# Two fused transformer blocks on one core: block 2's first layer norm and first feed-forward block by token tiles, the residual without GpSimd

## Chip, cores and metric

The kernel runs on 1 core of one Trainium2 chip. The metric is device time in microseconds of the whole kernel; less is better.

## What is computed

256 tokens of width 1024 go through two blocks. Block 1: RMS norm, stick-breaking attention and a short convolution, then a mixture of 32 experts. Block 2: attention (8 heads of 64) beside a gated MLP over positions, then a dense feed-forward, with a layer norm behind each of the two sums. The change touches the last lines of block 2:

```python
def swiglu_ffn(x, w_gate, w_up, w_down):
    return (jax.nn.silu(x @ w_gate) * (x @ w_up)) @ w_down
...
        mix = hybrid_mixer(x, w_in[l], attn_out_g[l], gmlp_out_g[l], gmlp_ln_g[l], gmlp_ln_b[l],
                           w_spatial[l], b_spatial[l], w_out[l])
        x = layer_norm(DEEPNORM_ALPHA * x + mix, ln1_g[l], ln1_b[l])
        ffn = swiglu_ffn(x, w_gate[l], w_up[l], w_down[l])
        x = layer_norm(DEEPNORM_ALPHA * x + ffn, ln2_g[l], ln2_b[l])
```

The feed-forward has 2816 hidden features, 22 blocks of 128.

## The kernel before

Everything is float32. A dense product is made of three: both operands are split into a rounded part and a rest (`hi_lo`, line 241: ACT copies into the rounded type, DVE subtracts), and PE adds hi*hi, hi*lo and lo*hi. The weights' halves are called `whi` and `wlo`, those of the activations `xh` and `xl`, `mh` and `ml`, `fh` and `fl`.

Weights come in tiles of one megabyte. `Feed` (line 48) lists them in the order of their use and issues the load of the next one on SP's queue as soon as a slot of the ring is free; `Split` (line 86) makes the halves a few units ahead into five buffers.

The stage of interest runs from line 1102 to the first feed-forward blocks. The 256 tokens are two tiles of 128 (`t` = 0, 1) with tokens on the partitions and the 1024 features on the free axis, in two halves of 512 (`c`). `attn_rows` (line 1105) gives the attention's part of the output projection for one tile, in units of 128 rows of the weight. `stats` (line 1121) adds it to the residual `xres` (`add_mix`), and takes mean and variance; POOL raises the variance to the power -0.5 (`rsqrt`, line 231). `normed` (line 1137) writes (x - mean) * rstd to `xn`, for tile 0 on ACT (which needs `mr`, the shifted mean, from DVE) and for tile 1 on DVE. PE transposes `xn` (`xn_t`), so that features come to the partitions, and `x3_t` applies gain and bias of the norm, which are per-partition scalars there, on ACT and DVE in turn. `hi_lo` then splits each chunk of 128 features over all 256 tokens, and `dense_feat` (line 258) multiplies it into the gate and the up block of the first 128 hidden features (`zg`, `zu`), chunk after chunk. `warm` (line 211) issues products that nothing reads.

The feed-forward needs the normed x once more as its own residual, by tokens. So POOL loads the four vectors of the two norms, spread over all partitions, with its own DMA queue (line 1191) and computes gain and bias on `xn` again into `xres` (lines 1193 and 1194):

```python
        for n, o in bc.items():
            nc.gpsimd.dma_start(out=o, in_=a[n].partition_broadcast(P))
        for t in range(NT):
            nc.gpsimd.tensor_tensor(out=xres[:, t, :], in0=xn[:, t, :], in1=bc["ln1_g"], op=ALU.mult)
            nc.gpsimd.tensor_tensor(out=xres[:, t, :], in0=xres[:, t, :], in1=bc["ln1_b"], op=ALU.add)
```

From there `hidden(f)` (line 1210) makes one block of 128 hidden features, gate and up, 24 products of 256 columns each, and `rows_proj` the down projection of two such blocks (`fdn`). At the end `last_rows`, `stats` and two passes on DVE give the second norm, tile by tile.

Inside `tc.manual_schedule` the engines named there keep the order of the source; what stands outside is placed by the scheduler, which may put an instruction ahead of ones written earlier.

Of the kernel before, what the change touches and what calls it, by code (L numbers as in the profile page):

```python
# [36 lines left out]
WARM3 = (6, 6)  # L37
# [10 lines left out]
class Feed:  # L48
    """Weight tiles of one megabyte each, loaded in the order of their use into the free slots."""
# [36 lines left out]
class Split:  # L86
    """Halves of weight tiles as hi + lo, made ahead of their use."""
# [28 lines left out]
def fused_blocks(ctx: ExitStack, tc: tile.TileContext, a, out):  # L116
# [28 lines left out]
    def in_halves(src):  # L145
        return [(slice(h * 1024, (h + 1) * 1024), src[:, h * 1024:(h + 1) * 1024]) for h in range(2)]

# [22 lines left out]
    for i in (2, 3, 0, 1):  # L170
        tiles(units_b, "wo2", [a["w_out_2"][i]])
    for i in range(12):
        if i < 11:
            tiles(units_b, "fgu", [a["w_ffn"][2 * i], a["w_ffn"][2 * i + 1]])
        if i:
            tiles(units_b, "fdn", [a["w_fdn"][i - 1]])

# [99 lines left out]
    def rows_proj(W, name, acc, xh, xl, k0, first, last, then={}):  # L277
        """acc[t][c] += x[:, two chunks from k0] @ w, w with 1024 columns."""
# [57 lines left out]
    def x_rstd(t):  # L336
        """1 / rms of a token tile of x, half of it on each engine."""
# [136 lines left out]
    def feat_pair(name, z):  # L474
        """z[128, 2, 256]: two blocks of 128 features of one projection."""
# [66 lines left out]
    with tc.manual_schedule(engines={mybir.EngineType.PE}):  # L542
# [31 lines left out]
        def x1_t(t, b):  # L574
            """Half b of x1 of token tile t as [d, tok]."""
# [28 lines left out]
    # what routing keeps per token goes where the router's weights were  # L604
# [62 lines left out]
    def first_max(vals, eq, nm):  # L667
        """One-hot of the first maximum along the last axis, into eq, and the maximum."""
# [13 lines left out]
    # the two best experts of each group, and the best group  # L682
# [33 lines left out]
    def gather(pg):  # L716
        """The tokens of a group of experts as [d, slots], normalised; some chunks of d at a time."""
# [16 lines left out]
    def scatter(g, pg):  # L734
        """[slots, tok]: the weight with which a slot's output goes to its token."""
# [13 lines left out]
    # the weights: softmax over the two experts, times the group's share  # L749
# [95 lines left out]
    # experts with more tokens than slots: the tokens beyond them, on all of the expert's weights  # L845
# [61 lines left out]
    def x2_tok(t, c):  # L907
        """ALPHA * x2 of token tile t, back as [tok, d]."""
# [80 lines left out]
    def soft_a(hp):  # L989
        """Scores with the mask, and their maxima."""  # L990
# [67 lines left out]
    def then(*steps):  # L1058
        """What follows a unit of weights: steps[i] after unit i."""
        return {i: (lambda fs=fs: [f(*a) for f, *a in fs]) for i, fs in enumerate(steps)}  # L1060
# [53 lines left out]
    # residual, layer norm  # L1114
# [3 lines left out]
    bc = {n: fp.tile([P, D], F32, name=n) for n in ("ln1_g", "ln1_b", "ln2_g", "ln2_b")}  # L1118
# [18 lines left out]
    def normed(t):  # L1137
        for c in range(2):
            cols = slice(c * 512, (c + 1) * 512)
            if t:  # L1140
                ts(xn[:, t, cols], xres[:, t, cols], *ln[t], op0=ALU.subtract, op1=ALU.mult)
            else:
                act(xn[:, t, cols], xres[:, t, cols], AF.Identity, scale=ln[t][1], bias=shift[t])

    with tc.manual_schedule(engines=in_order):
        zvs = [bank_c().rearrange("p (k s) -> p k s", k=2) for _ in range(4)]

        def xn_t(t, kc):
            tr(zvs[kc % 4][:, kc // 4, t * P:(t + 1) * P], xn[:, t, kc * P:(kc + 1) * P], ident)

        for c in range(2):
            attn_rows(0, (3,), (c,))
            stats(0, c, add_mix)
        attn_rows(1, (0, 1), (0, 1))
        W.ahead(W.n_got + 2)
        shift = {0: small(fp, 1, "mr")}
        stt(out=shift[0], in0=ln[0][0], scalar=-1.0, in1=ln[0][1], op0=ALU.mult, op1=ALU.mult)
        normed(0)
        for c in range(2):
            attn_rows(1, (2, 3), (c,))  # L1160
            stats(1, c, add_mix)
        warm(bank, WARM3[0], ident)
        for kc in range(KD):
            xn_t(0, kc)
        normed(1)
        warm(bank, WARM3[1], ident)
        x3 = {}

        def x3_t(kc):
            if kc >= KD:  # L1170
                return
            zv = zvs[kc % 4][:, kc // 4, :]
            x3[kc] = fp.tile([P, S], F32, tag="x3", name="x3", bufs=4)
            if kc % 2:
                act(x3[kc], zv, AF.Identity, scale=V("ln1_g", kc), bias=V("ln1_b", kc))
            else:
                ts(x3[kc], zv, V("ln1_g", kc), V("ln1_b", kc), op0=ALU.mult, op1=ALU.add)

        gate, up = W.get("fgu", 3), W.get("fgu", 4)
        zg, zu = bank()[:, 0:S], bank()[:, 0:S]  # L1180
        for kc in range(KD):
            xn_t(1, kc)
            if kc < 2:
                x3_t(kc)
        for kc in range(KD):
            hi_lo(xh[:, kc, :], xl[:, kc, :], x3[kc])
            x3_t(kc + 2)
            dense_feat(*gate, KD, xh, xl, zg, [kc])
            dense_feat(*up, KD, xh, xl, zu, [kc])
        for n, o in bc.items():  # L1190
            nc.gpsimd.dma_start(out=o, in_=a[n].partition_broadcast(P))
        for t in range(NT):
            nc.gpsimd.tensor_tensor(out=xres[:, t, :], in0=xn[:, t, :], in1=bc["ln1_g"], op=ALU.mult)
            nc.gpsimd.tensor_tensor(out=xres[:, t, :], in0=xres[:, t, :], in1=bc["ln1_b"], op=ALU.add)
        W.ahead(W.n_got + W.n)

# [20 lines left out]
    for i in range(12):  # L1217
        if i < 11:
# [4 lines left out]
            hidden(2 * i + 1)  # L1223
        if 0 < i < 10:
# [6 lines left out]
    # the last two pairs of chunks together, so that one half of the tokens is done early  # L1231
# [6 lines left out]

    for t in range(NT):
# [8 lines left out]
        mu, r = ln[t]  # L1248
        stt(out=xn[:, t, :], in0=xres[:, t, :], scalar=mu, in1=bc["ln2_g"], op0=ALU.subtract, op1=ALU.mult)
        for cols in (slice(0, 512), slice(512, 768), slice(768, D))[:2 + t]:  # L1250
            if not t:
                cols = slice(cols.start, cols.start + 512)
            o = xn[:, t, cols]
            stt(out=o, in0=o, scalar=r, in1=bc["ln2_b"][:, cols], op0=ALU.mult, op1=ALU.add)
# [8 lines left out]
def layout(i):  # L1263
    import numpy as np

    def chunks(w, n):
        """(K, F) -> (F/n, 128, K/128, n): column blocks, rows by partition."""
# [71 lines left out]
```

## Time and profile before

| | |
|---|---|
| runs | 716.70, 719.25, 719.62 us |
| median | 719.25 us |
| profiled execution | span 717.7 us (the page lists no other time for it) |
| PE busy | 665.7 us, 93% of the span |
| DVE busy | 343.9 us, 48% |
| ACT busy | 267.5 us, 37% |
| POOL busy | 58.1 us, 8% |
| mean granted clock of PE | 0.974 |

The share of an engine is a mean over stages with different limits, so what a stage waits for is read in that stage. A profile's timeline gives the start and the length of each instruction, in brackets the idle time of its engine before it and what ended that; a granted clock of 1.00 is 2.4 GHz on PE, 0.50 is 1.2 GHz. Ends of products on PE are modelled, so the distance of two starts tells more than the length of one.

### The profile page before, as it was taken

What the parts mean: (1) busy time and instruction counts of PE and PEld (TensorE: products, weight loads), DVE (VectorE), ACT (ScalarE), POOL (GpSimd) and SP (SyncE); (2) the same over time, 40 slices, a digit from 0 to 9 for tenths busy, and PEclk for the clock granted to TensorE, in tenths of its full rate; (3) what the DMA queues carried; (4) which work ended last, traced back from release to release, by engine and by line L of the source; (5) the groups of instructions that cost most, each with busy time, mean ns of one, the idle gap of its engine ahead of it and who ended that gap; (6) DMA issues with size and microseconds to landing.
All of it is one profiled execution on the core that took longest, in us unless ns stands there. A gap on an engine that the chain in (4) does not pass through costs nothing. (4 is left out here: it accounts for less than half of the span.)

```text
span 717.7 us, 11083 instructions
## 1 busy us (share of the span) xinstructions
PE 665.7 (93%) x4593; PEld 537.0 (75%) x4593; DVE 343.9 (48%) x532; ACT 267.5 (37%) x409; POOL 58.1 (8%) x68
## 2 busy tenths in 40 slices
PE   7999999999999889897799399999889999999995
PEld 6888999999964444442355288877789999999994
DVE  6657555555521220211000568676885555555556
ACT  6567554444310000000001564485554444444440
POOL 2321100000000000000000015101520000000001
PEclk9999999999999999999899799999979999999998
DMA  9983479639889999999999874632445555550001
GB/s 344 403 334 126 149 305 344 242 118 370 334 341 397 421 419 419 420 419 418 419 419 415 358 283 141 224 126 110 176 174 179 177 186 196 199 183 1 1 1 58
DMA packets 27560, 185.66 MB, mean 259 GB/s; under 512 B 3312, under 2 KB 3824, under 8 KB 5872
## 3 DMA queue, kind: packets, MB, share of 16 engines
q1 hardware_dynamic: 26928, 182.79, 65.7%
q0 software_dynamic: 576, 2.10, 0.8%
q8 instruction: 38, 0.62, 0.4%
q14 instruction: 18, 0.15, 0.1%
HBM read 183.83 MB, written 1.05 MB: 258 GB/s over the span
## 5 line engine op out<-in xcount | busy, mean ns | idle before, releaser
L243 DVE TENSOR_TENSOR wlo<-w,whi 128x1024 fp32r<-128x1024 f32 (+1 forms) x151 | 184.3, 1225 | 128.0 <-ACT whi L242 127.5
L242 ACT ACTIVATE whi<-w 128x1024 fp32r<-128x1024 f32 (+1 forms) x151 | 158.6, 1055 | 199.4 <-PE pa_t L255 75.0
L263 PE MATMUL pc_t<-xl,whi 128*128 128x256 f32 x464 | 132.2, 285 | 0.0
L262 PE MATMUL pc_t<-xh,whi 128*128 128x256 f32 x464 | 132.2, 285 | 0.0
L264 PE MATMUL pc_t<-xh,wlo 128*128 128x256 f32 x464 | 131.9, 285 | 0.0
L262 PEld LDWEIGHTS pc_t<-xh,whi 128*128 128x128 f32 x464 | 90.1, 194 | 0.4
L263 PEld LDWEIGHTS pc_t<-xl,whi 128*128 128x128 f32 x464 | 90.0, 194 | 0.4
L264 PEld LDWEIGHTS pc_t<-xh,wlo 128*128 128x128 f32 x464 | 89.8, 194 | 0.0
L780 PE MATMUL pc_t<-w,xg 128*32 128x512 f32 x512 | 62.0, 616 | 5.5 <-DMA w<-in_w_gu_dram 5.4
L810 ACT ACTIVATE h<-pc_t 128x256 f32<-128x256 f32 x8 | 3.1, 383 | 136.7 <-PE pc_t L729 112.0
L730 DVE TENSOR_TENSOR xg<-pc_t,vec 128x512 f32<-128x512 f32 (+2 forms) x18 | 11.4, 632 | 81.7 <-PE pc_t L729 81.7
L255 PE MATMUL pa_t<-whi,xh 128*128 128x512 f32 x112 | 44.8, 400 | 1.3 <-ACT xh L246 1.3
L780 PEld LDWEIGHTS pc_t<-w,xg 128*32 128x32 f32 x512 | 14.3, 111 | 40.8 <-issue 24.7
L255 PE MATMUL pa_t<-whi,xl 128*128 128x512 f32 x112 | 44.0, 392 | 0.0
L255 PE MATMUL pa_t<-wlo,xh 128*128 128x512 f32 x112 | 43.8, 391 | 0.0
L821 PEld LDWEIGHTS pa_t<-st,y 128*128 128x128 f32 x128 | 23.0, 189 | 21.9 <-DVE y L837 12.5
L821 PE MATMUL pa_t<-st,y 128*128 128x256 f32 x128 | 31.9, 392 | 6.3 <-DVE y L837 6.2
L263 PE MATMUL pa_t<-xl,whi 128*128 128x256 f32 x112 | 33.1, 295 | 5.0 <-DVE xl L243 4.9
L729 PEld LDWEIGHTS pc_t<-pr,xres 128*128 128x128 f32 x256 | 29.3, 192 | 8.4 <-PE pc_t L780 4.2
L780 PE MATMUL pc_t<-w,hT 128*32 128x512 f32 (+1 forms) x272 | 31.2, 574 | 4.1 <-ACT hT L816 4.1
L262 PE MATMUL pa_t<-xh,whi 128*128 128x256 f32 x112 | 32.8, 293 | 0.0
L264 PE MATMUL pa_t<-xh,wlo 128*128 128x256 f32 x112 | 32.4, 290 | 0.0
(296 smaller groups left out, 1042.0 us busy)
## 6 DMA issues: line engine op xcount, KB each, us to landing
w<-in_w_gu_dram SPq DMA_DIRECT2D x64, 1024.0 KB, 19.8
w<-in_w_dn_dram SPq DMA_DIRECT2D x32, 1024.0 KB, 19.9
w<-in_w_in_dram SPq DMA_DIRECT2D x28, 1024.0 KB, 14.5
w<-in_w_ffn_dram SPq DMA_DIRECT2D x22, 1024.0 KB, 5.0
w<-in_w_fdn_dram SPq DMA_DIRECT2D x11, 1024.0 KB, 5.0
w<-in_w_out_dram SPq DMA_DIRECT2D x8, 1024.0 KB, 6.1
w<-in_w_in_dram SPq DMA_DIRECT2D x4, 512.0 KB, 12.2
w<-in_w_cv_dram SPq DMA_DIRECT2D x2, 1024.0 KB, 9.6
```

What stands on the lines that cost most here:

```text
L242: act(hi, src, AF.Copy)
L243: tt(out=lo, in0=src, in1=hi.bitcast(F32), op=ALU.subtract)
L255: mm(acc[c], x_[:, kc, tok], w_[:, o + c * 512:o + (c + 1) * 512], start=first and i == 0 and n == 0, stop=last and i == len(ks) - 1 and n ...
L262: mm(acc, hi[:, f], xh[:, kc, :], start=kc == 0, stop=False)
L263: mm(acc, hi[:, f], xl[:, kc, :], start=False, stop=False)
L264: mm(acc, lo[:, f], xh[:, kc, :], start=False, stop=kc == nk - 1)
L729: mm(zv[:, k, :], xres[:, t, kc * P:(kc + 1) * P], pr[:, t, :], start=t == 0, stop=t == 1)
L730: tt(out=xg[:, ks, :], in0=zv, in1=V("ffn_g")[:, ks].unsqueeze(2).to_broadcast([P, n, P]), op=ALU.mult)
L780: mm(out[sl, 0:n], x[:, sl], w[:, e * 512 + i * n:e * 512 + (i + 1) * n], start=start, stop=stop, skip_group_check=True)
L810: act(h, gu[:, 0:256], AF.Silu)
L821: mm(acc[2 * c + k // 2][:, k % 2, :], ys[c][:, k * P:(k + 1) * P], st, start=False, stop=False, skip_group_check=True)
```

## The change

- The vectors of the norms come on SP's queue: two tiles of one megabyte, `ln1` (gain and bias) ahead of the first `fgu` tile and `ln2` behind the last `fdn` tile. `ln1` keeps its slot of the ring until its last use.
- POOL's four residual operations go. For tile 0, DVE does them (`xn` times gain, plus bias) in the loop of the feed-forward, written behind the second pass of that loop's `hidden` calls. For tile 1, DVE normalises by tokens: `centred` gives (x - mean) * gain into `xn`, `scaled` that times rstd plus bias, in quarters of 256 features, straight into `xres`; PE transposes `xres`, and no gain or bias is left to apply.
- Tile 0 is normalised on ACT as before and transposed between the two halves of tile 1's projection; gain and bias of its chunks are applied on ACT alone (`part0`).
- The first gate/up block is done for one token tile after the other (`first_hidden`, 128 columns a product): four pairs of chunks for tile 0, then four for tile 1.
- The products that nothing reads at this place (`WARM3`) go.
- The second norm's passes use the new helpers.

```diff
-WARM3 = (6, 6)
...
+    def on_all(g, b):
+        return [(slice(i * D, (i + 1) * D), a[n].partition_broadcast(P)) for i, n in enumerate((g, b))]
...
+    tiles(None, "ln1", [on_all("ln1_g", "ln1_b")])
     for i in range(12):
...
+    tiles(None, "ln2", [on_all("ln2_g", "ln2_b")])
...
+    def centred(t, cols, gain):
+        stt(out=xn[:, t, cols], in0=xres[:, t, cols], scalar=ln[t][0], in1=gain[:, cols],
+            op0=ALU.subtract, op1=ALU.mult)
+
+    def scaled(o, t, cols, bias):
+        stt(out=o, in0=xn[:, t, cols], scalar=ln[t][1], in1=bias[:, cols], op0=ALU.mult, op1=ALU.add)
...
+        W.ahead(W.n_got + 1)
         for c in range(2):
             attn_rows(0, (3,), (c,))
             stats(0, c, add_mix)
+        shift = small(fp, 1, "mr")
+        stt(out=shift, in0=ln[0][0], scalar=-1.0, in1=ln[0][1], op0=ALU.mult, op1=ALU.mult)
         attn_rows(1, (0, 1), (0, 1))
         W.ahead(W.n_got + 2)
-        shift = {0: small(fp, 1, "mr")}
-        stt(out=shift[0], in0=ln[0][0], scalar=-1.0, in1=ln[0][1], op0=ALU.mult, op1=ALU.mult)
-        normed(0)
-        for c in range(2):
-            attn_rows(1, (2, 3), (c,))
-            stats(1, c, add_mix)
-        warm(bank, WARM3[0], ident)
-        for kc in range(KD):
-            xn_t(0, kc)
-        normed(1)
-        warm(bank, WARM3[1], ident)
...
+        for cols in half:
+            act(xn[:, 0, cols], xres[:, 0, cols], AF.Identity, scale=ln[0][1], bias=shift)
+        attn_rows(1, (2, 3), (0,))
+        stats(1, 0, add_mix)
...
+        z0 = [turned(0, xn, k, 4) for k in (0, 4)]
+        attn_rows(1, (2, 3), (1,))
...
+        def part0(j):
+            x3 = fp.tile([P, 2, P], F32, tag="x3", name="x3", bufs=2)
+            for i in range(2):
+                kc = 2 * j + i
+                act(x3[:, i, :], z0[kc // 4][:, kc % 4, :], AF.Identity, scale=V("ln1_g", kc), bias=V("ln1_b", kc))
+            ks = slice(2 * j, 2 * j + 2)
+            hi_lo(xh[:, ks, tok[0]], xl[:, ks, tok[0]], x3)
+
+        def first_hidden(t, j):
+            for (hi, lo), z in ((gate, zg), (up, zu)):
+                for kc in (2 * j, 2 * j + 1):
+                    f = slice(kc * P, (kc + 1) * P)
+                    for n, (w_, x_) in enumerate(((hi, xh), (hi, xl), (lo, xh))):
+                        mm(z[:, tok[t]], w_[:, f], x_[:, kc, tok[t]], start=t == 0 and kc == 0 and n == 0,
+                           stop=kc == KD - 1 and n == 2, skip_group_check=True)
...
+        part0(0)
+        stats(1, 1, add_mix)
+        part0(1)
+        centred(1, half[0], g1)
+        part0(2)
+        centred(1, half[1], g1)
+        part0(3)
+        for j in range(4):
+            first_hidden(0, j)
+        z1 = []
+        for j in range(4):
+            scaled(xres[:, 1, quarter[j]], 1, quarter[j], b1)
+            z1.append(turned(1, xres, 2 * j, 2))
+            ks = slice(2 * j, 2 * j + 2)
+            hi_lo(xh[:, ks, tok[1]], xl[:, ks, tok[1]], z1[j])
+            if j:
+                first_hidden(1, j - 1)
+        first_hidden(1, 3)
         W.ahead(W.n_got + W.n)
...
             hidden(2 * i + 1)
+        if i == 1:
+            tt(out=xres[:, 0, :], in0=xn[:, 0, :], in1=g1, op=ALU.mult)
+            tt(out=xres[:, 0, :], in0=xres[:, 0, :], in1=b1, op=ALU.add)
+            feed.done(ln1)
```

`turned(t, src, k, n)` transposes n chunks of 128 features of a tile into one bank. The new lines shift the numbers: `add_mix` is L1139 in the changed kernel, the statistics L1130 to L1135, `hi_lo`'s subtraction L248, `first_hidden`'s products L1191, `centred` and `scaled` L1142 and L1146, tile 0's residual on DVE L1244 and L1245.

DVE in the changed kernel, from the first sum of token tile 1 to its `centred` (`w` is the tile with gain and bias, `x` a pair of chunks of tile 0):

```order
L1139 SCALAR_TENSOR_TENSOR xres<-pa_t,rs_34_5772,xres 128x512
L1244 TENSOR_TENSOR xres<-xn_5778,w 128x1024
L1130 BN_STATS bst<-xres 128x6
L248 TENSOR_TENSOR xl_4917<-x_5847,xh_4916 128x2x128
L1139 SCALAR_TENSOR_TENSOR xres<-pa_t,rs_34_5772,xres 128x512
L1245 TENSOR_TENSOR xres<-xres,w 128x1024
L1130 BN_STATS bst<-xres 128x6
L1133 BN_AGGR mv_5854<-bst 128x2
L1135 TENSOR_SCALAR ve_5856<-mv_5854 128x1
L248 TENSOR_TENSOR xl_4917<-x_5860,xh_4916 128x2x128
L1142 SCALAR_TENSOR_TENSOR xn_5778<-xres,mv_5854,w 128x512
```

The two residual operations of tile 0, written behind the second pass of the feed-forward loop, stand in the statistics of tile 1. In the kernel before, DVE has the same place without them:

```order
L1135 SCALAR_TENSOR_TENSOR xres<-pa_t,rs_34_5771,xres 128x512
L1126 BN_STATS bst<-xres 128x6
L1135 SCALAR_TENSOR_TENSOR xres<-pa_t,rs_34_5771,xres 128x512
L1126 BN_STATS bst<-xres 128x6
L1129 BN_AGGR mv_5844<-bst 128x2
L1131 TENSOR_SCALAR ve_5846<-mv_5844 128x1
L1141 TENSOR_SCALAR xn_5777<-xres,mv_5844,rs_41_5848 128x512 x2
L1177 TENSOR_SCALAR x_5877<-pc_t,vec 128x256
```

So two passes over 128x1024 moved in, and the first split of tile 0 (L248) moved ahead of tile 1's second sum.

PE in the kernel before, from the end of the projection to the first products of the gate block:

```order
L255 MATMUL pa_t<-whi,ml_4919 128x512
L215 MATMUL pa_t<-ident 128x128 x6
L1149 MATMUL pc_t<-ident,xn_5777 128x128 x8
L215 MATMUL pa_t<-ident 128x128 x6
L1149 MATMUL pc_t<-ident,xn_5777 128x128 x8
L262 MATMUL pa_t<-xh_4916,whi 128x256
```

and in the changed kernel, from tile 0's transposes on:

```order
L1169 MATMUL pc_t<-ident,xn_5778 128x128 x8
L260 MATMUL pa_t<-whi,mh_4918 128x512
L260 MATMUL pa_t<-wlo,mh_4918 128x512
L260 MATMUL pa_t<-whi,ml_4919 128x512
L260 MATMUL pa_t<-whi,mh_4918 128x512
L260 MATMUL pa_t<-wlo,mh_4918 128x512
L260 MATMUL pa_t<-whi,ml_4919 128x512
L1191 MATMUL pa_t<-xh_4916,whi 128x128
```

The transposes of tile 0 moved ahead of the last six products of the projection, the products that nothing reads are gone, and the gate block begins with tile 0 alone, at 128 columns.

## Rows read from the trace of the kernel before

**Rows 1.** span line; waits from 507 to 527: total us, times, longest

```profile
core 0 of [0], span 717.7 us
...
PE pa_t L263 <- DVE xl L243: 4.9, 4, 1.5
```

**Rows 2.** stretches: us, busy (count) of PE, PEld, DVE, ACT, POOL; PEclk, DMA, GB/s

```profile
516.70:520.17 3.47, 1.18 (x7) 0.98 (x8) 3.47 (x4) 2.27 (x4) 3.39 (x3) 1.00 0.26 107
520.17:530.41 10.24, 8.37 (x37) 7.78 (x37) 10.24 (x7) 4.96 (x6) 4.41 (x2) 0.50 0.21 62
```

**Rows 3.** timeline of PE: start us, us, instruction

```profile
517.81 0.28 PE L262 MATMUL pa_t<-xh,whi 128*128 128x256 f32 x1
517.92 0.28 PE L263 MATMUL pa_t<-xl,whi 128*128 128x256 f32 x1
...
520.41 0.41 PE L262 MATMUL pa_t<-xh,whi 128*128 128x256 f32 x1
520.62 0.41 PE L263 MATMUL pa_t<-xl,whi 128*128 128x256 f32 x1
...
526.22 0.41 PE L262 MATMUL pc_t<-xh,whi 128*128 128x256 f32 x1
```

**Rows 4.** timeline of POOL and DVE around the residual operations

```profile
514.76 2.36 POOL L1193 TENSOR_TENSOR xres<-xn,ln_g 128x1024 f32<-128x1024 f32 x1 [2.14 <-DMA ln_g<-in_ln_g_dram]
...
514.44 0.41 DVE L243 TENSOR_TENSOR xl<-x,xh 128x256 fp32r<-128x256 f32 x1
515.00 2.40 DVE L243 TENSOR_TENSOR xl<-x,xh 128x256 fp32r<-128x256 f32 x1 [0.15 <-ACT xh L242]
```

**Rows 5.** DVE's prices: timeline of the first norm; line 1254 (min/median/max ns)

```profile
502.79 0.73 DVE L1135 SCALAR_TENSOR_TENSOR xres<-pa_t,rs,xres 128x512 f32<-128x512 f32 x1
503.56 0.69 DVE L1126 BATCH_NORM_STATS2 bst<-xres 128x6 f32<-128x512 f32 x1
...
504.53 0.15 DVE L1131 TENSOR_SCALAR ve<-mv 128x1 f32<-128x1 f32 x1
504.60 1.22 DVE L243 TENSOR_TENSOR wlo<-w,whi 128x1024 fp32r<-128x1024 f32 x1
...
L1254 DVE SCALAR_TENSOR_TENSOR xn<-xn,rs,ln_b x5: 476/744/750, 707.4 to 713.9; 128x512 f32<-128x512 f32 x3, 128x256 f32<-128x256 f32 x2
```

**Rows 6.** timeline of POOL's power and of ACT's normed halves

```profile
500.31 0.55 POOL L233 TENSOR_TENSOR rs<-ms,mhalf 128x1 f32<-128x1 f32 x1 [3.93 <-DVE ms L238]
...
504.81 1.41 POOL L233 TENSOR_TENSOR rs<-ve,mhalf 128x1 f32<-128x1 f32 x1 [3.04 <-DVE ve L1131]
...
506.45 1.52 ACT L1143 ACTIVATE xn<-xres,mr,rs 128x512 f32<-128x512 f32 x2 [1.99 <-DVE mr L1157]
```

**Rows 7.** groups of ACT, 500 to 530: count, busy us, mean ns, idle before

```profile
L242 ACT ACTIVATE xh<-x 128x256 fp32r<-128x256 f32 x8 | 2.9, 409 | 2.4 <-DVE x L1177 2.4
```

**Rows 8.** timelines of PE and its weight loads (PEld): what sets the products' distance

```profile
505.70 0.39 PE L255 MATMUL pa_t<-whi,ml 128*128 128x512 f32 x1
...
508.62 1.04 PE L1149 MATMUL pc_t<-ident,xn 128*128 128x128 f32 x8
...
55.04 0.30 PEld L459 LDWEIGHTS pz_t<-spl,hi 128*128 128x128 f32 x2
...
187.61 1.51 PE L637 MATMUL pa_t<-wr,x1T 128*128 128x36 f32 x12
...
190.06 2.55 PE L215 MATMUL pc_t<-x1T,ident 128*128 128x128 f32 x11
```

**Rows 9.** stretches around 189.1, columns as in rows 2

```profile
185.70:189.10 3.40, 3.40 (x34) 3.40 (x33) 1.41 (x7) 3.35 (x9) 1.12 (x2) 1.00 1.00 381
189.10:192.50 3.40, 3.40 (x18) 3.40 (x18) 2.38 (x16) 0.22 (x2) 0.00 (x0) 0.50 1.01 422
192.50:195.90 3.40, 3.40 (x34) 3.32 (x34) 2.30 (x19) 0.21 (x1) 0.00 (x0) 1.00 0.47 195
```

**Rows 10.** timeline of SP's queue: the first loads of fgu tiles

```profile
437.19 15.31 SPq L72 DMA_DIRECT2D w<-in_w_ffn_dram  x4
```

More of the change, by code (lines that the diff above doesn't have):

```diff
@@ L1117, in fused_blocks @@
     xn = fp.tile([P, NT, D], F32, name="xn2")
-    bc = {n: fp.tile([P, D], F32, name=n) for n in ("ln1_g", "ln1_b", "ln2_g", "ln2_b")}
     ln = {}
@@ L1135, in add_mix @@
         stt(out=o, in0=acc[t][c], scalar=rs_a[t], in1=o, op0=ALU.mult, op1=ALU.add)
-    def normed(t):
-        for c in range(2):
[L1139 to L1143, printed above, removed]
+    def centred(t, cols, gain):
[3 more added lines that the diff above has]
+        stt(out=o, in0=xn[:, t, cols], scalar=ln[t][1], in1=bias[:, cols], op0=ALU.mult, op1=ALU.add)
+    tok = [slice(t * P, (t + 1) * P) for t in range(NT)]
+    half = [slice(0, 512), slice(512, D)]
+    quarter = [slice(i * 256, (i + 1) * 256) for i in range(4)]
     with tc.manual_schedule(engines=in_order):
-        zvs = [bank_c().rearrange("p (k s) -> p k s", k=2) for _ in range(4)]
-        def xn_t(t, kc):
-            tr(zvs[kc % 4][:, kc // 4, t * P:(t + 1) * P], xn[:, t, kc * P:(kc + 1) * P], ident)
+        W.ahead(W.n_got + 1)
         for c in range(2):
@@ L1153, in fused_blocks @@
             stats(0, c, add_mix)
+        shift = small(fp, 1, "mr")
+        stt(out=shift, in0=ln[0][0], scalar=-1.0, in1=ln[0][1], op0=ALU.mult, op1=ALU.mult)
         attn_rows(1, (0, 1), (0, 1))
         W.ahead(W.n_got + 2)
-        shift = {0: small(fp, 1, "mr")}
-        stt(out=shift[0], in0=ln[0][0], scalar=-1.0, in1=ln[0][1], op0=ALU.mult, op1=ALU.mult)
-        normed(0)
-        for c in range(2):
-            attn_rows(1, (2, 3), (c,))
-            stats(1, c, add_mix)
-        warm(bank, WARM3[0], ident)
@@ L1163, in fused_blocks @@
-        for kc in range(KD):
-            xn_t(0, kc)
-        normed(1)
-        warm(bank, WARM3[1], ident)
[L1167 to L1177, printed above, removed]
+        for cols in half:
+            act(xn[:, 0, cols], xres[:, 0, cols], AF.Identity, scale=ln[0][1], bias=shift)
@@ L1179, in fused_blocks, with turned @@
+        attn_rows(1, (2, 3), (0,))
+        stats(1, 0, add_mix)
+        def turned(t, src, k, n):
+            z = bank_c()[:, 0:n * P].rearrange("p (k s) -> p k s", k=n)
+            for i in range(n):
+                tr(z[:, i, :], src[:, t, (k + i) * P:(k + i + 1) * P], ident)
+            return z
+        z0 = [turned(0, xn, k, 4) for k in (0, 4)]
+        attn_rows(1, (2, 3), (1,))
         gate, up = W.get("fgu", 3), W.get("fgu", 4)
         zg, zu = bank()[:, 0:S], bank()[:, 0:S]
[L1181 to L1194, printed above, removed]
+        def part0(j):
[5 more added lines that the diff above has]
+            hi_lo(xh[:, ks, tok[0]], xl[:, ks, tok[0]], x3)
@@ new lines, in first_hidden @@
+        def first_hidden(t, j):
[5 more added lines that the diff above has]
+                           stop=kc == KD - 1 and n == 2, skip_group_check=True)
+        g1 = feed.get("ln1")
+        g1, b1, ln1 = g1[:, 0:D], g1[:, D:2 * D], g1
@@ L1237, in last_rows @@
         dense_tok(acc[t], ks[i][1], (c,), *ks[i][0], t, False, i == 1)
+    g2 = feed.get("ln2")
+    g2, b2_ = g2[:, 0:D], g2[:, D:2 * D]
     for t in range(NT):
@@ L1247, in fused_blocks @@
             stats(t, c, add_ffn)
[L1248 to L1254, printed above, removed]
+        centred(t, slice(0, D), g2)
+        for cols in [half[:2], [half[0], quarter[2], quarter[3]]][t]:
+            scaled(xn[:, t, cols], t, cols, b2_)
             store(t, cols)
```

## The prediction

> **What bounds the kernel now.** I read the page for the span, then the waits of PE, then the stretches around block 2's first layer norm, and last the instructions of each engine there. The span is 717.7 us, and between the output projection of block 2 and the feed-forward PE waits four times for DVE's `xl`, 4.9 us in all [rows 1]. The stretches show what follows: in 516.70 to 520.17 PE is busy 1.18 of 3.47 us, and from 520.17 to 530.41 its clock is at 0.50, the lower of its two levels (1.2 GHz) [rows 2]. A 256-column product then starts every 0.21 us, where it was 0.11 to 0.12 before [rows 3]. The cause is POOL: while its four residual operations of 2.4 us run, a subtraction on DVE that otherwise takes 0.41 takes 2.40 [rows 4]. The second feed-forward block (`hidden(1)`) starts at 526.22 [rows 3]; from there PE is bound by its own products, so what counts is when it starts, and at which clock. From 526.22 to 530.41 some 20 products lose 0.095 us each to the lower clock, 1.9 us: at the full clock the kernel would stand where it stands had `hidden(1)` started at 528.1.
>
> **The change part by part.** I keep the clock of the trace; up to 504.5 nothing that PE waits for is moved.
>
> *Vectors through SP.* POOL loses four DMA issues. SP gets two loads ahead of the `fgu` tiles and two behind the last `fdn` tile. The first pair holds one slot of the ring, so every later load goes out with the issue of its successor. The four `fgu` issues that begin at 437.19 last 15.31 us [rows 10], so the first `fgu` tile is still issued by 452.5, some 50 us before block 0 reads it. Cost 0; without that lead, a load would stand in front of `hidden(0)`.
>
> *POOL's residual operations become DVE's.* The source places L1244 and L1245 behind `hidden(3)`, but they stand outside the hand-ordered part, and DVE's order has them earlier: L1244 ahead of the statistics of token tile 1's first half, L1245 ahead of those of its second. Each is a two-input pass over 128x1024; the nearest row is `wlo` with 1.22 us [rows 5]. Both are on the path to tile 1's norm: 2.4 us. L1244 also waits for ACT's second normed half; behind it on DVE stand the statistics and the first `xl` of tile 0, which PE waits for.
>
> *Start of the stage.* `mr` now stands ahead of `wlo`, so POOL's power takes 0.55 and not the 1.41 that it takes beside `wlo` [rows 6]: `mr` at 505.4, ACT's two halves (1.52) done at 507.15. DVE: `wlo` 505.5 to 506.7, `add_mix` 0.73 [rows 5], L1244 507.3 to 508.5, statistics 0.69, `xl` of the first two chunks 0.41: 509.5. PE ends tile 1's first half with the product of 505.70 [rows 8] at 505.9, waits for ACT, does eight transposes to 507.6 (0.11 each, [rows 8]) and six 512-column products to 509.0. The 24 warm records are gone, 2.7 us of PE that covered waits.
>
> *First block by token tiles.* 48 products of 256 columns become 96 of 128. A weight load of the same type is followed by the next 0.11 us later, though its product has only 128 columns (0.30 for two loads of 0.19 each, [rows 8]), and even 36-column products are 0.11 apart (1.51 for twelve, each 0.28 long, [rows 8]). So 96 take 10.6 us against 5.7: 4.9 more on PE. The Trainium skill ("TensorE: Matmul & The Clock Gate", Back-to-back issue gap) gives some 81 ns for a sustained 128-column product; by it an estimate would be 7.8 us. The rows are slower and decide.
>
> *Path at the full clock.* Chunks 0 and 1 of tile 0: 12 products, 509.5 to 510.85. The next `xl` stands on DVE behind `add_mix` (from 509.4), L1245, the statistics up to `ve` (1.12 from 503.56 to 504.68, [rows 5]): 512.65. **PE idles 1.8 us.** Then two `centred` at 0.74, two `xl`, and POOL's power, which must find a place between them (0.45): 515.1. PE does the other 36 products until 516.8. Tile 1 starts with a round: transposes 0.5 with their landing, ACT's `xh` 0.41 [rows 7], `xl` 0.41, `scaled` 0.48 [rows 5], until PE may go on at 518.5: **1.6 us idle** again. From there PE is the bound: 48 products and six transposes, 6.0 us, and some hops: `hidden(1)` at 525.2, so 1.0 earlier than now, and 2.9 with the 1.9 of the lower clock.
>
> *The clock.* It decides, and no row shows this very mix; I bound it from both sides. Nothing falls: 2.9 us gained. The clock falls in the idle time and stays down until wide products come: the rows nearest are these. Before the fall at 520.17 PE stood still between its products, seven of them in 3.47 us [rows 2]. Before the fall at 189.1 it was busy all 3.40 us, with 34 products, most of 36 columns [rows 8, 9]: a queue of narrow products without a gap did not hold the clock either. In the changed stage both come together: from 509.0 to 518.4 PE has 48 products of 128 columns and two idle times. I take the fall, between 512 and 515.
>
> At 0.50 a 128-column product comes every 0.213 us (2.55 for eleven of 0.42, [rows 8]), so token halves then cost twice what they cost above, and no 256-column product shares the load. With the fall at 512.7: 36 products 7.7 us, to 520.4; the round with slower transposes 2.2; 48 products and six transposes 11.5: `hidden(1)` at 533.9 to 534.1. With the fall at 515 it is 532.2. In the trace the clock came back 4.2 us after `hidden(1)` had begun (530.41 after 526.22, [rows 2, 3]), at a loss of 1.9; I allow 1.0 to 2.8. Against 528.1 that is 532.2 + 1.0 to 534.1 + 2.8, so +5.1 to +8.8; I take +6.5, a little under the middle (6.9), since an early fall and a late return are the less likely pair.
>
> **The sum.** 717.7 + 6.5 = 724.2 us of span. The page gives no other time for the profiled execution; the median of the runs, 719.25, is 1.55 above the span. On it: 725.7 us. The end of the kernel (second norm) keeps its operations, and its vectors lie ready.
>
> **Rivals.**
>
> *The clock holds.* Then only the 2.9 us count: 716.3. For it: both idle times stay under 2 us, PE's queue is otherwise full, and the blocking by POOL is gone. The same Trainium skill page (Why this matters for your kernels) asks only that no long idle gap stand between bursts, and by that rule this would be the case. Against it: single waits of at most 1.5 us [rows 1] were enough for the fall at 520.17, and at 189.1 there was none. The point from which it decides is the first idle time, 511 to 512.7: if that leaves 1.00, this rival has won.
>
> *A short fall.* The clock falls but returns within the token halves, because they follow without a gap at the lower clock. 36 products then lose 0.1 us each and the round 0.6: 4.3 us, less 2.9: 720.7. For it: 128-column products without a gap (the eleven of [rows 8]) stood in the stretch at 0.50 after which the clock was 1.00 again [rows 9]. Against it: those are plain float32 products, two records each, and say little of these.
>
> *The hoisted operations cost more.* If L1244 waited for its vector, PE would idle from 509 on. The load is 50 us early; I give it no chance of its own.
>
> **How the numbers follow.** Fall that lasts: 0.58, short fall 0.17, clock holds 0.25. A measurement of this kernel tells about 0.5% (3.6 us) from no change. The lasting fall is slower almost wholly (0.56), the short one nearly always the same (0.02 slower), the held clock ends 2.9 us below: faster 0.09, same 0.16. So faster 0.09, same 0.33, slower 0.58. The likeliest case alone is 724.0 to 728.0; the range of eight in ten also takes in the other two, down to 715.0, 1.3 under the held clock's 716.3 because the two idle times are worked out to about that.
>
> **What would show it.** Right: no `xl` of 2.4 us; L1244 and L1245 at 1.2 us between the statistics; an idle PE of about 1.8 and 1.6 us; the clock at 0.50 from 512 to 515 on until some us into `hidden(1)`; L1191 products 0.21 apart; `hidden(1)` near 533. Wrong: PEclk 1.00 through 511 to 519, or products of 128 columns at less than 0.2 us while it reads 0.50.

## The result, and the profile after

The changed kernel takes 723.29 us (median of 6 runs), the kernel before 718.8 us (6 runs, three of them new): the ratio is 1.007, 95% interval 1.0049 to 1.009, so 5.0 us slower by the ratio (3.5 to 6.5; the medians lie 4.5 apart). The forecast was 725.7 us, slower.

The span of the profiled execution rose by 3.1 us, from 717.7 to 720.8. That understates the change: at the start of the stage the changed kernel was 1.79 us ahead, although nothing is changed there (the first of the products that the timeline names `one,roped`, within the output projection, starts at 499.53 before and at 497.74 now). In the execution before, PE's clock was at 0.50 from 189.1 to 192.5 [rows 9]; in this one it was not. This start moves with the execution in the other kernels too (496.98 to 501.67 in the table below). I therefore measure the stage by **D**, the time from that product to the first product of the down projection (`whi,fh`), both from the timeline of PE: 45.8 us before, 51.0 now, so +5.2, in agreement with the runs. From there to the end both kernels take 172 us.

The waits of PE in the stage, after (total us, times, longest), answer to [rows 1]:

```profile
core 0 of [0], span 720.8 us
...
PE pa_t L1191 <- DVE xl L248: 1.8, 2, 1.6
...
PE pc_t L1169 <- DVE xres L1146: 1.4, 1, 1.4
```

PE waits 3.2 us here, 1.8 of them for DVE's `xl` and 1.4 for tile 1's `scaled`, where it was 4.9. The waits became shorter, and yet the kernel is slower. The stretches say why (columns as in [rows 2]):

```profile
509.10:512.51 3.41, 1.80 (x17) 1.67 (x16) 3.34 (x9) 1.23 (x3) 0.66 (x1) 1.00 0.01 2
512.51:516.87 4.36, 4.36 (x23) 4.36 (x22) 0.67 (x2) 0.00 (x0) 0.00 (x0) 0.50 0.00 0
516.87:519.24 2.37, 0.95 (x5) 0.58 (x6) 0.82 (x2) 0.38 (x1) 0.00 (x0) 0.50 0.00 0
519.24:530.20 10.96, 10.96 (x54) 10.96 (x53) 5.47 (x8) 5.22 (x8) 0.00 (x0) 0.50 0.31 102
530.20:532.99 2.79, 2.79 (x14) 2.79 (x15) 1.96 (x4) 2.74 (x4) 0.00 (x0) 0.50 0.92 335
532.99:536.40 3.41, 3.41 (x31) 3.41 (x30) 2.06 (x3) 1.33 (x2) 0.00 (x0) 1.00 0.80 329
```

The clock reads 1.00 until 512.51, 0.50 from there to 532.99, and 1.00 behind it: 20.5 us at the low level, 10.2 before [rows 2]. The timeline of PE shows the two gaps, and the distance of products in between:

```profile
508.96 0.27 PE L1191 MATMUL pa_t<-xh,whi 128*128 128x128 f32 x1
510.84 0.33 PE L1191 MATMUL pa_t<-xl,whi 128*128 128x128 f32 x1 [1.61 <-DVE xl L248]
...
512.81 0.41 PE L1191 MATMUL pa_t<-xh,wlo 128*128 128x128 f32 x1
513.03 0.41 PE L1191 MATMUL pa_t<-xh,whi 128*128 128x128 f32 x1
...
516.87 0.65 PE L1169 MATMUL pc_t<-ident,xres 128*128 128x128 f32 x2
518.93 0.66 PE L1169 MATMUL pc_t<-ident,xres 128*128 128x128 f32 x2 [1.42 <-DVE xres L1146]
...
530.20 0.52 PE L267 MATMUL pc_t<-xh,whi 128*128 128x256 f32 x1
```

PE stands from the product of 508.96 (which ends by 509.23) to 510.84, and again from the end of the two transposes of 516.87 (517.52) to 518.93. From 512.6 on, the products of 128 columns come every 0.21 us (512.81 to 513.03); `hidden(1)` starts at 530.20. The DVE rows ahead of the first gap show the two residual passes of tile 0 within the statistics of tile 1:

```profile
505.48 1.22 DVE L1244 TENSOR_TENSOR xres<-xn,w 128x1024 f32<-128x1024 f32 x1
506.61 0.69 DVE L1130 BATCH_NORM_STATS2 bst<-xres 128x6 f32<-128x512 f32 x1
507.21 0.41 DVE L248 TENSOR_TENSOR xl<-x,xh 128x256 fp32r<-128x256 f32 x1
507.54 0.74 DVE L1139 SCALAR_TENSOR_TENSOR xres<-pa_t,rs,xres 128x512 f32<-128x512 f32 x1
508.20 1.22 DVE L1245 TENSOR_TENSOR xres<-xres,w 128x1024 f32<-128x1024 f32 x1
509.33 0.69 DVE L1130 BATCH_NORM_STATS2 bst<-xres 128x6 f32<-128x512 f32 x1
...
510.37 0.42 DVE L248 TENSOR_TENSOR xl<-x,xh 128x256 fp32r<-128x256 f32 x1
```

No `xl` of 2.4 us is left, as there was in [rows 4]. Between the sum of 507.54 and the `xl` of 510.37, for which PE waits, stand L1245 with 1.22 us and the statistics.

### The profile page after: what moved, and what is told of

Read it like the earlier page. It is cut to its first block, busy times and chain, and to the rows that moved or that the text cites. A ratio compares the mean times of both kernels' runs of the same rounds, so it can differ in the third digit from the quotient of the medians.

```text
span 720.8 us, 11136 instructions
## 1 busy us (share of the span) xinstructions
PE 673.0 (93%) x4617; PEld 545.4 (76%) x4617; DVE 338.7 (47%) x534; ACT 269.1 (37%) x413; POOL 45.0 (6%) x60
## 5 line engine op out<-in xcount | busy, mean ns | idle before, releaser
L248 DVE TENSOR_TENSOR wlo<-w,whi 128x1024 fp32r<-128x1024 f32 (+1 forms) x151 | 184.8, 1228 | 129.3 <-ACT whi L247 128.8
L734 PE MATMUL pc_t<-pr,xres 128*128 128x128 f32 x256 | 32.1, 284 | 0.9 <-DVE pr L725 0.9
L842 DVE COPY y<-pc_t 128x512 f32<-128x512 f32 x7 | 4.8, 692 | 50.8 <-PE pc_t L785 50.8
L260 PE MATMUL pa_t<-whi,fh 128*128 128x512 f32 x88 | 28.5, 391 | 0.0
```

The lines of the kernel that those rows point to most:

```text
L248: tt(out=lo, in0=src, in1=hi.bitcast(F32), op=ALU.subtract)
L734: mm(zv[:, k, :], xres[:, t, kc * P:(kc + 1) * P], pr[:, t, :], start=t == 0, stop=t == 1)
```

## The experiments

The table has D and its parts for all kernels (starts from the timeline of PE in each profile, us), and the measured ratio to the kernel before with its interval; each ratio is taken against runs of the kernel before from the same session, whose medians were 717.9 to 718.8 us.

| kernel | `one,roped` | `hidden(1)` | `whi,fh` | D | median | ratio |
|---|---|---|---|---|---|---|
| before | 499.53 | 526.22 | 545.33 | 45.8 | 718.8 | 1 |
| after | 497.74 | 530.20 | 548.75 | 51.0 | 723.29 | 1.007 (1.0049 to 1.009) |
| e1_no_hoist | 498.13 | 528.71 | 548.00 | 49.9 | 720.8 | 1.0031 (1.0014 to 1.0049) |
| e2_warm | 500.03 | 528.15 | 545.50 | 45.5 | 718.29 | 0.9995 (0.9979 to 1.0012) |
| e5_fill | 499.81 | 525.10 | 542.46 | 42.7 | 715.79 | 0.9947 (0.9927 to 0.9967) |
| e6_fill_first | 496.98 | 525.96 | 544.15 | 47.2 | 719.56 | 1.0012 (0.9988 to 1.0036) |
| e4_no_idle | 501.67 | 523.98 | 541.33 | 39.7 | 711.4 | 0.9899 (0.9879 to 0.9919) |
| e7_joint | 499.35 | 522.57 | 539.85 | 40.5 | 713.96 | 0.9935 (0.9909 to 0.9961) |
| e3_before_dve | 497.11 | 516.16 | 533.44 | 36.3 | 709.93 | 0.9881 (0.9859 to 0.9903) |
| e8_pool_late | 499.45 | 518.48 | 535.75 | 36.3 | 708.86 | 0.9854 (0.9831 to 0.9877) |
| e9_before_sp | 497.85 | 516.88 | 534.16 | 36.3 | 708.22 | 0.9857 (0.9826 to 0.9889) |
| e10_unpinned | 497.11 | 518.53 | 537.13 | 40.0 | 712.16 | 0.9915 (0.9884 to 0.9945) |

### Is it the hoisted passes or the clock?

```diff
 # e1_no_hoist, against the changed kernel
-            tt(out=xres[:, 0, :], in0=xn[:, 0, :], in1=g1, op=ALU.mult)
-            tt(out=xres[:, 0, :], in0=xres[:, 0, :], in1=b1, op=ALU.add)
+            tc.keep_in_program_order(tt(out=xres[:, 0, :], in0=xn[:, 0, :], in1=g1, op=ALU.mult))
+            tc.keep_in_program_order(tt(out=xres[:, 0, :], in0=xres[:, 0, :], in1=b1, op=ALU.add))
```

> The changed kernel with tile 0's two residual passes kept on DVE where they are written, behind hidden(3). Measure of the stage: D, from the first L1055-type product (one,roped) to the first fdn product (whi,fh): 45.8 us before, 51.0 after. Theory (clock): the passes lengthen only the first idle time of PE; without them it shrinks from 1.6 to 0.9 us, the second one of 1.4 us stays, the clock still falls to 0.50 between 512 and 516 and stays there until 256-column products come. D 49 to 51, time 721 to 723.5. Rival (the two hoisted passes are the cost): the clock holds, D 44, time near 716.

D is 49.9, as the theory had it, 1.1 us shorter than in the changed kernel; the median is 2.5 us lower, just under the theory's 721. The clock falls in the same place, though the first gap is now 1.21 us from start to start and not 1.88, some 0.9 of it idle (stretches, columns as before):

```profile
509.30:512.71 3.41, 2.56 (x23) 2.56 (x23) 3.12 (x9) 1.23 (x3) 0.66 (x1) 1.00 0.02 10
512.71:516.12 3.41, 3.32 (x17) 2.92 (x15) 0.00 (x0) 0.06 (x1) 0.00 (x0) 0.50 0.00 0
```

So by D the hoist is a fifth of the loss, and by the medians about half; why the two differ stays open (D is read from one execution, and the profiled executions of the two kernels, 722.74 and 721.73 us, lie 1.0 apart). Either way the kernel is still slower than the one before, and to take the hoist out does not save the clock.

```diff
 # e2_warm, against the changed kernel; e5_fill has 8 and 6 in place of 16 and 12
         for j in range(4):
             first_hidden(0, j)
+            if j == 0:
+                warm(bank, 16, ident)
...
             z1.append(turned(1, xres, 2 * j, 2))
+            if j == 0:
+                warm(bank, 12, ident)
```

> The changed kernel with 16 products that nothing reads behind the first pair of chunks of tile 0 and 12 behind the first transposes of tile 1, so that PE is busy in both idle times; the hoisted passes stay. Theory (idle time between narrow products fells the clock): it stays at 1.00, hidden(1) starts about 522.5 and not 530.2, D 42 to 43, time 714 to 715. Rival (128-column products keep the clock down or fell it whatever stands between them): the clock falls in the same place, D 51 or more, time 723 or more.

The theory held on the clock, which stayed at 1.00, and missed on the time: D is 45.5, not 42 to 43. The two fillings in the timeline of PE:

```profile
511.26 3.79 PE L220 MATMUL pa_t<-ident 128*128 128x128 f32 x32
...
519.10 2.84 PE L220 MATMUL pa_t<-ident 128*128 128x128 f32 x24
```

A plain float32 product is two records of 0.11 us, so 28 of them (32 and 24 records) took 6.6 us where 3.0 were idle (1.6 and 1.4). Half as many, then:

> As e2_warm with half the products: 8 behind the first pair of chunks and 6 behind the first transposes. A plain float32 product of 128 columns shows as two records of 0.11 us, so e2_warm's 28 took 6.6 us (3.79 and 2.84) where about 3.3 us of idle time were to be filled; these take 1.9 and 1.4. Theory: clock stays at 1.00, D falls from e2_warm's 45.5 by the 3.3 us to 42 to 42.5, time 714 to 715.5; what the fall of the clock costs the changed kernel is then after minus this, 8 to 9 us of D. Rival (the filling has to be longer than the idle time): the clock falls, D 50 to 51, time 722 to 723.

```profile
511.04 2.00 PE L220 MATMUL pa_t<-ident 128*128 128x128 f32 x16
...
517.12 1.50 PE L220 MATMUL pa_t<-ident 128*128 128x128 f32 x12
```

```profile
513.20:517.20 4.00, 4.00 (x38) 4.00 (x38) 2.05 (x5) 0.92 (x3) 0.07 (x1) 1.00 0.00 0
517.20:521.00 3.80, 3.69 (x33) 3.39 (x31) 1.63 (x4) 0.86 (x3) 0.00 (x0) 1.00 0.00 0
```

The clock stays, the fillings take 2.0 and 1.5 us, D is 42.7 and the median 715.79, both a little above the theory's 42.5 and 715.5. The same kernel with the same products of 128 columns is thus 8.4 us of D shorter (7.5 by the medians) once PE is kept busy in two gaps of 3.0 us together. That is what the fall of the clock costs. The stretches are of one execution each, but the difference is in all runs: the mean granted clock of a whole execution is 0.965 to 0.971 in the six runs of the changed kernel, 0.967 to 0.974 in the twelve of e1_no_hoist, and 0.980 to 0.987 in the twelve of e5_fill.

```diff
 # e6_fill_first, against e5_fill
             z1.append(turned(1, xres, 2 * j, 2))
-            if j == 0:
-                warm(bank, 6, ident)
```

> As e5_fill with the first filling alone: the idle time of 1.4 us between the token tiles stays. Theory (each idle time between narrow products suffices): the clock falls between 516 and 521, tile 1's products are 0.21 us apart, D 46 to 48, time 718 to 721. Rival (only the first idle time, behind six 512-column products and one pair, fells it): the clock stays, D 42 to 42.5, time 714 to 715.5.

```profile
514.17:517.68 3.51, 2.05 (x18) 1.71 (x17) 1.64 (x4) 0.77 (x2) 0.00 (x0) 1.00 0.00 0
517.68:521.10 3.42, 3.42 (x18) 3.42 (x18) 0.82 (x2) 0.38 (x1) 0.00 (x0) 0.50 0.13 29
```

With the second gap alone left open, the clock falls behind that gap; D is 47.2. The 12 runs of this kernel lie between 714.25 and 722.63 us, wider apart than those of any other changed kernel, and their mean granted clocks between 0.971 and 0.982; two of them (714.25 and 716.29 us) reach the 0.980 that every run of e5_fill has. So the gap seems to fell the clock in most executions and not in all. Only one of them has a profile, so that reading is not shown.

### Do narrow products fell the clock by themselves?

```diff
 # e4_no_idle, against e1_no_hoist
         part0(0)
-        stats(1, 1, add_mix)
         part0(1)
-        centred(1, half[0], g1)
+        stats(1, 1, add_mix)
         part0(2)
-        centred(1, half[1], g1)
+        centred(1, half[0], g1)
+        scale1(0)
         part0(3)
-        for j in range(4):
+        centred(1, half[1], g1)
+        scale1(1)
+        for j in range(3):
             first_hidden(0, j)
+        z1.append(turned(1, xres, 0, 2))
+        first_hidden(0, 3)
+        split1(0)
...
```

(`scale1` and `split1` are the `scaled` and the `hi_lo` of one quarter; the other quarters follow as in the changed kernel, each transposed ahead of the products of the one before it.)

> The changed kernel without the hoist and with the stage in another order: second split of tile 0 ahead of tile 1's second statistics, tile 1's first quarter scaled and transposed ahead of the last products of tile 0, so that PE should not wait while it does the 96 products of 128 columns; no product added. Theory (idle time is needed for the fall): the clock stays at 1.00, hidden(1) starts near 519, D 38 to 40, time 710 to 712. Rival (a queue of 128-column products fells the clock without any idle time): the clock falls during tile 0 or tile 1, the products are 0.21 us apart from there on, D 45 to 49, time 718 to 722.

```profile
511.19:514.60 3.41, 3.14 (x28) 3.00 (x27) 2.77 (x7) 2.70 (x8) 0.55 (x1) 1.00 0.52 219
514.60:518.01 3.41, 3.17 (x30) 3.06 (x29) 2.58 (x6) 0.38 (x1) 0.11 (x1) 1.00 0.01 2
518.01:521.43 3.42, 3.35 (x30) 3.07 (x29) 1.63 (x4) 0.77 (x2) 0.00 (x0) 1.00 0.00 0
521.43:523.98 2.55, 2.55 (x26) 2.55 (x25) 1.50 (x2) 2.43 (x4) 0.00 (x0) 1.00 0.02 6
```

No product is added, and 96 products of 128 columns run at 1.00 for 12.8 us. PE is busy 92 to 100% of these stretches; no two of its products start more than 0.54 us apart. D is 39.7, the median 711.4. The rival falls: at 128 columns the width alone does not bring the clock down.

### What was the split by token tiles worth?

```diff
 # e7_joint, against e4_no_idle: each pair of chunks for both token tiles at once
-        def first_hidden(t, j):
-...
+        def first_hidden(j):
+            for (hi, lo), z in ((gate, zg), (up, zu)):
+                dense_feat(hi, lo, KD, xh, xl, z, (2 * j, 2 * j + 1))
...
+        warm(bank, 18, ident)
...
+        warm(bank, 4, ident)
```

> e4_no_idle with the first gate/up block over both token tiles again (48 products of 256 columns, each pair behind tile 1's split of it) and 22 products that nothing reads where PE would wait. Theory (the split by token tiles buys nothing, since a product of 128 columns takes 0.11 us and one of 256 takes 0.12): hidden(1) starts where e4_no_idle has it or up to 1.5 us earlier, D 38 to 40, time 709.5 to 711.5. Rival (the early start on tile 0 is what covers the norm of tile 1): D 42 to 44, time 714 to 716.

Neither: D is 40.5, just over the theory's 40, and the median is 2.6 us above that of e4_no_idle, though the intervals of the two ratios still overlap (0.9909 to 0.9961, 0.9879 to 0.9919). So the early start on tile 0 covers about as much as the narrow products cost; in this order of the norm the split is worth 0.8 us by D and 2.6 by the medians. But the order itself is late. The second sum of tile 1 on DVE, first in e3_before_dve (below), which keeps the old order, then in e7_joint:

```profile
505.31 0.73 DVE L1135 SCALAR_TENSOR_TENSOR xres<-pa_t,rs,xres 128x512 f32<-128x512 f32 x1
```

```profile
509.75 0.75 DVE L1139 SCALAR_TENSOR_TENSOR xres<-pa_t,rs,xres 128x512 f32<-128x512 f32 x1
```

From `one,roped` that is 8.2 us (505.31 - 497.11) and 10.4 (509.75 - 499.35). In the new order the last six products of the projection stand behind the transposes of tile 0 and their wait for ACT, and two splits of tile 0 stand ahead of the sum.

The clock stays at 1.00 in e7_joint, although PE stands idle for 0.67 and 0.53 us, each time behind filling products:

```profile
513.72 0.41 PE L1169 MATMUL pc_t<-ident,xres 128*128 128x128 f32 x2 [0.67 <-DVE xres L1146]
...
515.55 0.41 PE L1169 MATMUL pc_t<-ident,xres 128*128 128x128 f32 x2 [0.53 <-DVE xres L1146]
```

### Which part would have helped?

```diff
 # e3_before_dve, against the kernel before
-        for t in range(NT):
-            nc.gpsimd.tensor_tensor(out=xres[:, t, :], in0=xn[:, t, :], in1=bc["ln1_g"], op=ALU.mult)
-            nc.gpsimd.tensor_tensor(out=xres[:, t, :], in0=xres[:, t, :], in1=bc["ln1_b"], op=ALU.add)
...
             hidden(2 * i + 1)
+        if i in (1, 2):
+            t = i - 1
+            tc.keep_in_program_order(tt(out=xres[:, t, :], in0=xn[:, t, :], in1=bc["ln1_g"], op=ALU.mult))
+            tc.keep_in_program_order(tt(out=xres[:, t, :], in0=xres[:, t, :], in1=bc["ln1_b"], op=ALU.add))
```

> The kernel before with one edit: the four residual passes go from POOL to DVE, two behind hidden(3), two behind hidden(5); vectors still by POOL's queue, first gate/up block still over both token tiles. Theory (POOL's passes were what blocked the stage before): every xl takes 0.41 us, the 4.9 us of waits and the fall of the clock at 520 go, hidden(1) starts 8 to 10 us earlier, D 36 to 38, time 709 to 711. Rival (the work only moves: 4.9 us of DVE in the feed-forward delay the weights' halves): D as in the theory, but PE waits for wlo behind it, time 713 to 716. Rival (the norm's chain, not POOL, sets the pace): D 44 to 46, time 717 to 719.

```profile
513.00:516.16 3.16, 3.16 (x29) 3.16 (x27) 2.51 (x6) 2.97 (x6) 0.00 (x0) 1.00 0.81 300
516.16:520.17 4.01, 4.01 (x36) 4.01 (x35) 4.01 (x5) 3.99 (x4) 0.00 (x0) 1.00 0.39 101
```

The theory held: PE is busy without a gap at 1.00 through the first block, `hidden(1)` starts 19.05 us behind `one,roped` (26.69 before, 32.46 after; so 7.6 us earlier than before, a little less than the 8 to 10 expected), D is 36.3. This one part of the change, put where DVE has time, makes the kernel 1.2% faster.

```diff
 # e8_pool_late, against e3_before_dve: the four passes on POOL again, behind
+        if f == 1:
+            late = small(fp, 1, "late")
+            tc.keep_in_program_order(nc.gpsimd.tensor_tensor(out=late, in0=s[:, 0:1], in1=s[:, 0:1], op=ALU.mult))
...
```

> The kernel before with POOL's four residual passes kept on POOL, behind one POOL operation of one column that reads hidden(1)'s activation, so that they run in the feed-forward and not in the first gate/up block. Theory (the place of POOL's passes was the fault, not the engine): every xl takes 0.41 us, D 36 to 37; in the feed-forward some of DVE's wlo take 2.4 us and more, but DVE has slack there: time 709 to 711, as e3_before_dve. Rival (POOL blocks DVE wherever it runs, and the weights' halves come late): PE waits for wlo in the feed-forward, time 712 to 716.

First the stretch of the four passes in the feed-forward (columns as before), then two of them on POOL and three of DVE's operations beside them:

```profile
525.96:538.86 12.90, 12.90 (x97) 12.37 (x97) 11.76 (x7) 5.50 (x8) 12.74 (x5) 1.00 0.50 187
```

```profile
527.02 2.59 POOL L1226 TENSOR_TENSOR xres<-xn,ln_g 128x1024 f32<-128x1024 f32 x1
...
536.39 2.47 POOL L1227 TENSOR_TENSOR xres<-xres,ln_b 128x1024 f32<-128x1024 f32 x1
...
528.35 2.35 DVE L243 TENSOR_TENSOR wlo<-w,whi 128x1024 fp32r<-128x1024 f32 x1 [1.01 <-ACT whi L242]
...
531.17 2.89 DVE L243 TENSOR_TENSOR wlo<-w,whi 128x1024 fp32r<-128x1024 f32 x1
...
536.52 3.42 DVE L243 TENSOR_TENSOR wlo<-w,whi 128x1024 fp32r<-128x1024 f32 x1
```

The blocking is still there: two-input passes on DVE that take 1.22 us alone take 2.35 to 3.42. PE does not feel it, busy 12.90 of 12.90 us, because DVE makes the weights' halves ahead of their use there. So the fault of the kernel before was the place of POOL's passes and not the engine. The Trainium skill ("SBUF — State Buffer", section "SBUF: two separate sides") says that DVE and GpSimd share one pair of ports as an exclusive lock, and that an operation of DVE with two inputs contends for it with one of GpSimd that reads SBUF. These rows agree, with 2.35 to 3.42 us beside POOL against 1.22 alone.

```diff
 # e9_before_sp, against e3_before_dve
...
+    tiles(None, "ln1", [on_all("ln1_g", "ln1_b")])
     for i in range(12):
...
+    tiles(None, "ln2", [on_all("ln2_g", "ln2_b")])
...
-        for n, o in bc.items():
-            nc.gpsimd.dma_start(out=o, in_=a[n].partition_broadcast(P))
+        ln1 = feed.get("ln1")
+        bc["ln1_g"], bc["ln1_b"] = ln1[:, 0:D], ln1[:, D:2 * D]
...
```

> e3_before_dve with the change's other part that had been costed at nothing: the vectors of both norms as two tiles on SP's queue instead of four loads by POOL. Theory: no difference to e3_before_dve, D 36 to 37, time 708.5 to 711. Rival (the first tile holds a slot of the ring and the weights come late): PE waits for weights behind the first gate/up block, time 712 or more.

D is 36.3 again; the interval of the ratio overlaps that of e3_before_dve. The vectors' way costs nothing, as the prediction had it.

e10_unpinned is e3_before_dve without the two `keep_in_program_order`:

> e3_before_dve with the four residual passes left to the scheduler: three of them now stand between the splits xl of the first gate/up block, each 1.22 us on DVE's chain. Theory (a pass hoisted into the chain that PE waits for costs its length less PE's slack, and the clock if the waits are enough): PE waits about 0.7 to 1.0 us three times, D 38.5 to 39.5 if the clock stays, 43 to 46 if it falls; time 711 to 713, or 715 to 718. Rival (DVE has slack in the first block): D 36 to 37, time 709 to 711.

```profile
510.66 0.42 DVE L243 TENSOR_TENSOR xl<-x,xh 128x256 fp32r<-128x256 f32 x1
512.35 1.23 DVE L1223 TENSOR_TENSOR xres<-xn,ln_g 128x1024 f32<-128x1024 f32 x1 [1.28 <-DMA ln_g<-in_ln_g_dram]
513.50 0.42 DVE L243 TENSOR_TENSOR xl<-x,xh 128x256 fp32r<-128x256 f32 x1
...
511.82 0.28 PE L262 MATMUL pa_t<-xh,whi 128*128 128x256 f32 x1
513.97 0.39 PE L263 MATMUL pa_t<-xl,whi 128*128 128x256 f32 x1 [1.87 <-DVE xl L243]
```

D is 40.0, between the two cases of the theory: PE waits once, from 511.82 to 513.97, and not three times. The scheduler had put the first pass between two `xl`, and there it waited 1.28 us for its vector, which POOL's queue had only just loaded, and then took 1.23. The clock fell behind this wait, for 3.4 us, and came back:

```profile
510.00:514.58 4.58, 2.63 (x19) 2.22 (x19) 3.30 (x7) 2.06 (x6) 0.20 (x1) 1.00 0.99 347
514.58:517.99 3.41, 3.41 (x18) 3.30 (x17) 3.41 (x6) 2.33 (x6) 0.00 (x0) 0.50 0.23 94
517.99:521.40 3.41, 3.41 (x30) 3.41 (x30) 3.41 (x6) 3.41 (x5) 0.00 (x0) 1.00 0.02 5
```

Passes that nobody needs before the second norm cost 3.7 us of D, the fall among it, where the scheduler put them.

## Why the prediction was right

*The stage's steps.* L1244 and L1245 take 1.22 us each in the statistics, as written. The idle times came as forecast: 1.6 us where 1.8 was worked out, and 1.4 where it was 1.6. The products of 128 columns are 0.11 us apart at the full clock (in e4_no_idle twelve start from 521.75 to 522.97), 0.21 at the low one. The 81 ns that the Trainium skill gives for them ("TensorE: Matmul & The Clock Gate", Back-to-back issue gap) are not reached here.

*The clock.* It fell at 512.51, which on the scale of the kernel before is 514.3 (1.79 later), within the 512 to 515 forecast. It stayed down through both token tiles and came back 2.8 us into `hidden(1)`; the rival of a short fall is out, since PE did products of 128 columns without a gap from 519.24 to 530.20 and the clock did not rise.

*The sum.* `hidden(1)` at 530.20 is 532.0 on the scale of before, just under the 532.2 to 534.1; tile 1's products and transposes, taken as 11.5 us, took 10.96. Behind it 13 products lost 0.095 us each, 1.2, in the range of 1.0 to 2.8. So 532.0 + 1.2 - 528.1 = +5.1, with D at +5.2, where +6.5 was taken. **The mis-sized term** is the clock's: of +5.1 to +8.8 the prediction took 6.5, "since an early fall and a late return are the less likely pair", and what came was a late fall with an early return, the other end. That the return came early is in part chance: the low level lasted 2.8 us into `hidden(1)` here, 4.5 in e1_no_hoist and 2.0 in e6_fill_first. The forecast lies 2.4 us above the median: 1.3 are this term, 0.45 the median of the kernel before, which came down from 719.25 to 718.8, and the rest is not explained.

*A rival's price.* For the clock that holds the prediction had 2.9 us gained; e5_fill, which is that case, has D 3.15 shorter than before, and 0.9947 (3.8 us).

*The reason that failed.* The fall was argued from two rows together: gaps, and narrow products that without a gap "did not hold the clock either" [rows 8, 9]. The second half does not carry over: those had 36 columns, and in ten of the twelve profiles the clock did not fall behind them (below); with 128 columns e4_no_idle held 1.00. The gaps were the cause here; e5_fill and e6_fill_first show it from both sides. So the fall came for one of the two reasons given; as far as the chance of 0.58 rested on the other, it was luck. Of the Trainium skill's rule ("TensorE: Matmul & The Clock Gate", Why this matters for your kernels), that long idle gaps between bursts are to be avoided, the prediction noted that gaps under 2 us would pass. The runs speak against that reading: gaps of 0.9 (e1_no_hoist), 1.4 and 1.6 us between products of 128 columns were each followed by a fall. The 0.67 and 0.53 us of e7_joint, between products of other kinds, were not; no run varies the length of one gap alone.

*What the prediction did not weigh.* Removing POOL's passes alone was worth 9.5 us of D. The changed kernel gets this gain and spends it: on twice as many products in the first block (4.9 us by the prediction's working), on tile 1's second sum, which starts 9.8 us behind `one,roped` (507.54 - 497.74) and not 8.2, and on the clock (8.4). These overlap and are not to be added up to a tenth of a microsecond.

## What to carry to other kernels

Halving the columns of a product does not halve its time here (0.11 us for 128 columns, 0.12 for 256), so a split that starts early doubles the work of that block, and it must cover at least as much waiting. Look at what stands in the gaps of PE before removing products that nothing reads: 3.5 us of filling in 3.0 us of idle time were worth 7.5 us. (No run puts the removed products back in their old place.) When an operation is moved off a blocked engine, pin it where its new engine has slack; a scheduler may put it back on the path.

The best versions keep the old order of the stage and only move the four residual passes into the feed-forward, on DVE (e3_before_dve, e9_before_sp) or on POOL (e8_pool_late). They take 708.2 to 709.9 us, 1.2 to 1.5% below the kernel before; these runs do not tell the three apart.

## What the runs showed that I had not expected

The same products hold one level of the clock and do not bring back the other: with 128 columns, 1.00 stayed for 12.8 us in which PE was never idle for more than 0.27 us (e4_no_idle), and 0.50 stayed for 11.0 us without a gap (after, 519.24 to 530.20). In `hidden(1)`, with 256 columns, 1.00 came back after 2.8 us, after 4.5 in e1_no_hoist and after 2.0 in e6_fill_first (the stretches at 0.50, first e1_no_hoist, then e6_fill_first):

```profile
528.70:533.19 4.49, 4.49 (x23) 4.49 (x23) 3.22 (x5) 2.75 (x4) 0.00 (x0) 0.50 0.97 358
```

```profile
525.96:527.92 1.96, 1.96 (x10) 1.96 (x11) 1.65 (x3) 1.95 (x3) 0.00 (x0) 0.50 0.79 255
```

The number of columns is not all of it: in the kernel before, plain float32 products of 128 columns stood in the 3.4 us behind which the clock was 1.00 again [rows 8, 9]. For the split products of this stage, at least, it pays not to enter a run of narrow ones through a gap.

The clock can fall in an unchanged stage in one execution and not in another: the fall near 189 is in the profiles of the kernel before and of e4_no_idle, and in none of the other kernels'. The 18 products from 189.1 to 192.5, against 34 in the same time before them [rows 9], make some 1.6 us of delay by an estimate (16 products at 0.1). Even without that fall `one,roped` starts anywhere from 496.98 to 500.03, so two profiles are better compared from a common instruction on than by their spans.
